# Routing of a product-key expert layer: one span of gather slots for each head, a second buffer for transposed h, and w_out's products in smaller steps through the gather's row buffers

## The chip, the cores and the metric

The kernel runs on one core of a Trainium2 chip, as one launch. The metric is the device time of that launch in microseconds (us), as the median of several executions. One execution was also profiled; the rows in this document come from it.

## The reference, cut to what matters

256 tokens (two tiles of 128) of 1024 channels go through two layers. Each layer mixes the tokens in four ways (short convolution, latent attention, a 31-tap convolution, windowed attention), multiplies by `w_out`, normalises to `h`, and then sends every token to 128 of 16384 experts:

```python
m = per_head_rms_norm(concat[shortconv, MLA, conformer_conv, swa](x @ W_in))
h = layer_norm(ALPHA * x + m @ W_out)
x = layer_norm(ALPHA * h + PEER(h))

def PEER(xc):                                   # 8 heads, 16 experts a head and token
    q = (xc @ w_q).reshape(c, 8, 2, 128)
    sc = einsum('chpd,hpnd->chpn', q, sub_keys)             # two times 128 scores
    top_s, top_i = top_k(sc, 16)
    best_s, best_j = top_k(top_s[:, :, 0, :, None] + top_s[:, :, 1, None, :], 16)
    idx = the expert of each best pair
    gate = softmax(best_s)
    act = gelu(einsum('chkd,cd->chk', u_tab[idx], xc))
    return einsum('chk,chkd->cd', gate * act, v_tab[idx])
```

All of it is float32.

## The kernel before, in words

**The gather.** `u` and `v` of an expert lie side by side in a row of 2048 floats. For each tile of each layer (a stage: four in all, `todo`) the function `peer` (L734) runs 128 *slots*, 16 for each head. A slot gathers 128 rows, one for each token: 1 MB by an indirect DMA that GpSimd (POOL) issues (L756) into one of ten row buffers (`ROWS`, tag `row`). VectorE (DVE) multiplies the u half with `h` and sums (L759), ScalarE (ACT) takes the gelu, the gate and a diagonal matrix `dg` (L741 to L744), and TensorE (PE) adds `dg` times the v half to two accumulators `acc` (L746). `post` of a slot is written after the DVE step of the next slot. A row buffer is free when PE has read it.

**The routing.** `route` (L660) makes the 16 experts and gates of one head: two times eight products `ps_q` of transposed `h` with the head's weights `w_q_t` (1152 KB), a product `ps_rs` with the keys, then top-16 searches and index arithmetic on DVE (`top16`, `sum_grid`, `experts`). Heads 0 to 2 keep their weights from the first tile to the second in `held0` to `held2`; heads 3 and 4 are loaded for each tile; heads 5 to 7 are loaded once and routed for both tiles in one go (`joint`, L797). For that the transposed `h` of the first tile is made a second time, in the buffer `pT`, and the second tile begins its gather with heads 5 to 7.

**The mixers.** `mixer` (L286) makes `h` of one tile. At its end `outs` (L572) loads four blocks of `w_out` (1 MB each) and makes 16 products `ps_o` (L586), and a layer norm follows. Weights go through the pool `wp` of three buffers, filled by SP's DMA queue in the order in which a scheduler puts the loads.

**Who sets the order.** `paced` (L822) emits the slots of a stage one after another, and between them steps of other *tasks*. A task is a generator with a first and a last slot and a cost; each `yield` says what it has spent, and a task is stepped until it has spent its share for the slot. `main_loop` (L866) lists the tasks of each stage: routing in rows such as `(joint(0), 65, 100, ...)`, which means that six routes (three heads for two tiles) are spread over slots 65 to 100, and mixers such as `(mix(1, 1), 4, 66, MIX)`. `keep_behind` ties the two streams together: on PE, DVE and ACT a task's step comes at most six slots before or behind its place. The order within that is a scheduler's.

The stages are, with the tasks beside the gather:

| stage | gather of | routing beside it, slots | mixer beside it, slots |
|---|---|---|---|
| 1 | layer 1, tile 1 | head 1: 0-4; heads 2 to 4: 4-17; joint 5 to 7: 65-100 | layer 1, tile 2: 0-65 |
| 2 | layer 1, tile 2 | heads 0 to 4: 2-36; next layer's 0, 1: 104-120 | layer 2, tile 1: 36-104 |
| 3 | layer 2, tile 1 | heads 2 to 4: 3-17; joint 5 to 7: 66-101 | layer 2, tile 2: 4-66 |
| 4 | layer 2, tile 2 | heads 0 to 4: 2-70 | none |

(The code counts layers and tiles from 0.) Ahead of stage 1 lie the first mixer and the first route; behind stage 4 the last layer norm.

Of the kernel before, what the change touches and what calls it, by code (L numbers as in the profile page):

```python
# [61 lines left out]
def kernel(ctx: ExitStack, tc: tile.TileContext, x, positions, w_in, w_att, bcast, perch, lnrows, lncols,  # L62
# [597 lines left out]
    def route(l, hd, hTs):  # L660

        n = QK
        if hd in HELD and 1 in hTs:
            w = held.pop(hd)
        else:
            if hd in HELD:
                held[hd] = rp.tile([P, n], F32, tag=f"held{hd}", name="w_q_t")
            w = load_w(w_qk, (l * NH + hd) * P * n, n, "w_q_t", held.get(hd))
        wq = w[:, :KC * 256].rearrange("p (c n) -> p c n", c=KC)
        for t, hT in hTs.items():  # L670
            s = []
            for j in range(2):
                ps = pm.tile([P, P], F32, tag="mm", name="ps_q")
                for c in range(KC):
                    nc.tensor.matmul(ps, wq[:, c, j * P:(j + 1) * P], hT[:, c, :], start=(c == 0), stop=(c == KC - 1))  # L675
                yield 1.8
                qT = sp.tile([P, P], F32, tag=f"rq{j}", name="rq", bufs=1)
                S.copy(qT, ps)  # L678
                ps = pm.tile([P, P], F32, tag="mm", name="ps_rs")
                nc.tensor.matmul(ps, qT, w[:, KC * 256 + j * P:KC * 256 + (j + 1) * P], start=True, stop=True)  # L680
                s.append(sp.tile([P, P], F32, tag=f"rsc{j}", name="rsc", bufs=1))
                S.copy(s[j], ps)  # L682
                yield 0.3
            bs = sp.tile([P, TOPK], F32, tag="bs", name="bs")
            bj = sp.tile([P, TOPK], U32, tag="bj", name="bj")
            ix8 = None
            if (l, t, hd) == (0, 0, 0):

                t8 = sp.tile([P, 2, TOPK], F32, tag="tv", name="t8")
                i8 = sp.tile([P, 2, TOPK], U32, tag="ti", name="i8")  # L690
                for j in range(2):
                    V.max(t8[:, j, 0:8], s[j])
                    V.max_index(i8[:, j, 0:8], t8[:, j, 0:8], s[j])
                c8 = sum_grid(t8, 8)
                b8 = sp.tile([P, 8], F32, tag="b8", name="b8", bufs=1)
                j8 = sp.tile([P, 8], U32, tag="j8", name="j8", bufs=1)
                V.max(b8, c8)
                V.max_index(j8, b8, c8)
                ix8 = gp.tile([P, 8], I32, tag="ix8", name="ix8", bufs=1)
                experts(l, ix8, j8, i8, 8, 8)  # L700
            tv = sp.tile([P, 2, TOPK], F32, **(dict(tag="ex0", bufs=1) if (l, t) == (0, 0) and hd < HS else dict(tag="tv")),
                         name="tv")
            ti = sp.tile([P, 2, TOPK], U32, tag="ti", name="ti")
            for j in range(2):
                top16(tv[:, j, :], ti[:, j, :], s[j])
                yield 1.0
            top16(bs, bj, sum_grid(tv, TOPK))
            yield 2.0
            ix = gp.tile([P, TOPK], I32, tag=f"ix{hd}", name="ix", bufs=2)
            experts(l, ix, bj, ti, TOPK, TOPK)  # L710
            yield 2.2

            nb = sp.tile([P, 1], F32, tag="nb", name="nb")
            V.tensor_scalar(nb, bs[:, 0:1], -1.0 / 16, None, op0=ALU.mult)
            th = sp.tile([P, TOPK], F32, tag="th", name="th")
            S.activation(th, bs, AF.Tanh, bias=nb, scale=1.0 / 16)
            tm = sp.tile([P, TOPK], F32, tag="tm", name="tm")
            V.tensor_scalar(tm, th, -1.0, 1.0, op0=ALU.mult, op1=ALU.add)
            V.reciprocal(tm, tm)
            V.scalar_tensor_tensor(tm, th, 1.0, tm, op0=ALU.add, op1=ALU.mult)  # L720
            sm = sp.tile([P, 1], F32, tag="gsm", name="gsm")
            gate = gp.tile([P, TOPK], F32, tag=f"gate{hd}", name="gate", bufs=2)
            S.activation(tm, tm, AF.Square)
            S.activation(tm, tm, AF.Square)
            S.activation(gate, tm, AF.Square, accum_out=sm)
            V.reciprocal(sm, sm)
            V.tensor_scalar(gate, gate, sm, None, op0=ALU.mult)
            R[l, t, hd] = (ix8, ix, gate)
            yield 0.5
# [56 lines left out]

    def solo(l, t, heads):

        if t == 0 and not hot["pT"]:
            hot["pT"] = transpose8(H[l, 0], "hT0", "pT")  # L790
            yield 1.5
        for hd in heads:
            yield from route(l, hd, {t: hot["T"] if t else hot["pT"]})
        if t == 0 and hd == HS - 1:
            hot["pT"] = 0

    def joint(l):  # L797

        hot["T"] = transpose8(H[l, 1], "hT1", "T")
        yield 1.5  # L800
        hT0 = transpose8(H[l, 0], "hT0", "pT")
        yield 1.5
        for hd in range(HS, NH):
            yield from route(l, hd, {0: hT0, 1: hot["T"]})
# [164 lines left out]
```

## Time and profile before

| what | value |
|---|---|
| time before, median of 3 runs (lowest to highest) | 1544.36 us (1543.88 to 1546.22) |
| the profiled execution's own time | 1543.23 us |
| its span, first to last instruction | 1541.2 us |
| busy: PE, DVE, POOL, ACT | 87%, 71%, 40%, 38% |
| moved by DMA | 614.47 MB, 399 GB/s over the span |
| of this the gather | 512 indirect DMAs, 536.90 MB |

Busy shares are means over stretches that have different limits. [...]

### The profile page before, as it was taken

How to read it: one execution, taken by the hardware profiler on the slowest of the kernel's cores; microseconds unless marked ns; L12 is line 12 of the kernel's file. 1: busy time of each engine (PE TensorE's matmuls, PEld its weight loads, DVE VectorE, ACT ScalarE, POOL GpSimd, SP SyncE). 2: the span in 40 equal slices, each digit the busy share in tenths (PEclk: the TensorE clock that was granted, in tenths of full speed). 3: DMA queues.
4: the chain of work that ended last, by engine and by line, in shares of the span. 5: the costliest groups of instructions: out<-in, count | busy, mean ns of one | idle time of the engine just before them, and what ended most of it. 6: DMA issues, size and time to landing. Idle time of an engine off the chain costs nothing.

```text
span 1541.2 us, 17548 instructions
## 1 busy us (share of the span) xinstructions
PE 1345.3 (87%) x4868; PEld 720.2 (47%) x4868; DVE 1096.8 (71%) x3163; ACT 589.6 (38%) x2047; POOL 618.4 (40%) x539
## 2 busy tenths in 40 slices
PE   8999889798989789978989999898988898888776
PEld 8676444454335455533444665444543444432222
DVE  6789785699659775677487787757984777665445
ACT  4234442343434333354243334423443343433332
POOL 2044233234654233434335334232445454555551
PEclk9999899999999999999999999899999999999999
DMA  9579999999999999999999999999999999999995
GB/s 381 195 319 421 418 393 401 416 385 405 420 421 422 422 422 423 422 422 384 424 381 422 422 423 422 378 420 363 374 396 422 421 422 421 421 421 422 421 421 239
DMA packets 86209, 614.47 MB, mean 399 GB/s; under 512 B 10337, under 2 KB 10721, under 8 KB 12769
## 3 DMA queue, kind: packets, MB, share of 16 engines
q0 software_dynamic: 73728, 536.90, 84.9%
q1 hardware_dynamic: 12096, 76.44, 12.1%
q8 instruction: 40, 0.66, 0.2%
q14 instruction: 57, 0.46, 0.1%
q10 hardware_dynamic: 288, 0.01, 0.0%
HBM read 612.26 MB, written 1.05 MB: 398 GB/s over the span
## 4 chain that ended last, share of the span: by engine, by line
PE 39%; DMA 28%; DVE 22%; issue 6%; ACT 4%; POOL 0%; DVEq 0%; SPq 0%; POOLq 0%
DMA row<-in_uv_dram,ix 27%; PE acc L746 26%; DVE row L759 9%; PE ps_q L675 5%; PE ps_o L586 3%; DVE cv L510 1%; DMA w_in_t<-in_w_in_dram 1%; ACT dg L744 1%; PE ps_mla L320 1%; DVE bj L655 1%; DVE rsc L656 1%; DVE ti L655 1%; DVE grid L656 1%; DVE ti L658 1%; ACT act L742 1%
## 5 line engine op out<-in xcount | busy, mean ns | idle before, releaser
L746 PE MATMUL acc<-row,dg 128*128 128x512 f32 x2048 | 987.2, 615 | 162.0 <-ACT dg L744 160.8
L756 POOL DMA_INDIRECT row<-in_uv_dram,ix x512 | 607.4, 1186 | 866.0 <-PE acc L746 299.4
L759 DVE SCALAR_TENSOR_TENSOR row<-row,h 128x1024 f32<-128x1024 f32 x512 | 619.2, 1219 | 225.8 <-DMA row<-in_uv_dram,ix 201.2
L746 PEld LDWEIGHTS acc<-row,dg 128*128 128x128 f32 x2048 | 366.1, 193 | 643.7 <-ACT dg L744 331.9
L741 ACT ACTIVATE act<-act 128x1 f32<-128x1 f32 x512 | 103.1, 201 | 581.5 <-DVE row L759 580.7
L744 ACT ACTIVATE dg<-idn,act 128x128 f32<-128x128 f32 x512 | 205.1, 401 | 72.5 <-PE acc L746 58.5
L742 ACT ACTIVATE act<-act,gate 128x1 f32<-128x1 f32 x512 | 150.2, 294 | 15.5
L675 PEld LDWEIGHTS ps_q<-hT,w_q_t 128*128 128x128 f32 x1024 | 124.6, 194 | 23.3 <-issue 22.2
L675 PE MATMUL ps_q<-hT,w_q_t 128*128 128x128 f32 x1024 | 128.6, 278 | 5.8 <-DVE hp L153 5.6
L510 DVE SCALAR_TENSOR_TENSOR cv<-cfu,pc,cv 128x128 f32<-128x128 f32 x217 | 68.7, 358 | 0.9
L586 PE MATMUL ps_o<-w_out_t,mT 128*128 128x512 f32 x128 | 61.7, 615 | 1.7 <-DVE mT L370 1.7
L654 DVE MAX8 tv<-rsc 128x8 f32<-128x128 f32 x64 | 18.4, 289 | 46.8 <-ACT rsc L682 46.5
L682 ACT COPY rsc<-ps_rs 128x128 f32<-128x128 f32 x64 | 17.0, 265 | 66.7 <-PE ps_rs L680 66.4
L759 DVE DVE_READ_ACCUMULATOR row<-row,h 128x1 f32 x512 | 41.9, 82 | 0.0
L586 PEld LDWEIGHTS ps_o<-w_out_t,mT 128*128 128x128 f32 x128 | 24.7, 198 | 31.2 <-issue 28.7
L680 PEld LDWEIGHTS ps_rs<-w_q_t,rq 128*128 128x128 f32 x128 | 23.6, 190 | 29.4 <-issue 22.2
L592 DVE SCALAR_TENSOR_TENSOR hp<-x,ps_o 128x512 f32<-128x512 f32 x8 | 5.5, 687 | 38.5 <-PE ps_o L586 38.5
L678 ACT COPY rq<-ps_q 128x128 f32<-128x128 f32 x64 | 16.8, 262 | 39.7 <-PE ps_q L675 39.5
L680 PE MATMUL ps_rs<-w_q_t,rq 128*128 128x128 f32 x128 | 25.1, 278 | 2.1 <-ACT rq L678 2.1
L320 PEld LDWEIGHTS ps_mla<-w_in_t,xT 128*128 128x128 f32 x128 | 23.4, 196 | 4.0 <-issue 2.9
L320 PE MATMUL ps_mla<-w_in_t,xT 128*128 128x208 f32 x128 | 24.9, 348 | 0.2 <-DMA w_in_t<-in_w_in_dram 0.2
L649 DVE TENSOR_REDUCE ex<-grid 128x32 f32<-128x512 f32 (+1 forms) x33 | 22.0, 667 | 0.3
(215 smaller groups left out, 977.9 us busy)
## 6 DMA issues: line engine op xcount, KB each, us to landing
w_in_t<-in_w_in_dram SPq DMA_DIRECT2D x24, 1024.0 KB, 10.1
w_q_t<-in_w_qk_dram SPq DMA_DIRECT2D x20, 1152.0 KB, 9.4
w_out_t<-in_w_out_dram SPq DMA_DIRECT2D x16, 1024.0 KB, 10.4
row<-in_uv_dram,ix POOLq DMA_INDIRECT x512, 16.5
w_in_t<-in_w_in_dram SPq DMA_DIRECT2D x6, 832.0 KB, 7.9
att<-in_w_att_dram SPq DMA_DIRECT2D x2, 640.0 KB, 12.7
x<-in_x_dram SPq DMA_DIRECT2D x2, 512.0 KB, 6.7
gb<-in_lnrows_dram SPq DMA_DIRECT2D x1, 1024.0 KB, 13.6
```

Source lines behind the costliest of these rows:

```text
L320: nc.tensor.matmul(ps, xT[:, c, :], w[:, c, a:b], start=(c == 0), stop=(c == KC - 1))
L510: V.scalar_tensor_tensor(cv[j], src, wt, cv[j], op0=ALU.mult, op1=ALU.add)
L586: nc.tensor.matmul(po[j], mixed_T()[:, 2 * g + c, :], wg[:, c, j * 512:(j + 1) * 512], start=(n == 0 and c == 0), stop=(n == 3 and c == 1))
L655: V.max_index(idx[:, 0:8], val[:, 0:8], s)
L675: nc.tensor.matmul(ps, wq[:, c, j * P:(j + 1) * P], hT[:, c, :], start=(c == 0), stop=(c == KC - 1))
L680: nc.tensor.matmul(ps, qT, w[:, KC * 256 + j * P:KC * 256 + (j + 1) * P], start=True, stop=True)
L741: S.activation(act, act, AF.Gelu)
L742: S.activation(act, act, AF.Copy, scale=gate[:, k % TOPK:k % TOPK + 1])
L744: S.activation(dg, idn, AF.Copy, scale=act)
L746: nc.tensor.matmul(acc[j], dg, row[:, DM + j * 512:DM + (j + 1) * 512], start=(k == 0), stop=(k == n - 1))
L756: nc.gpsimd.indirect_dma_start(out=row, out_offset=None, in_=uv, in_offset=bass.IndirectOffsetOnAxis(ap=ix[:, k % TOPK:k % TOPK + 1], axis=0))
L759: V.scalar_tensor_tensor(row[:, :DM], row[:, :DM], 1.0, h, op0=ALU.mult, op1=ALU.mult, accum_out=act)
```

## The change

- `route` takes one tile and one head. `joint` and `solo` are gone. Each head of each tile is a task of its own with its own span of slots. In stages 1 and 3 the first tile's heads follow each other at some 16 slots each, the mixer beside them; from slot 80 the second tile's heads 5 to 7 and the first tile's head 7 follow.
- The weights of heads 5 to 7 are kept in the three `wp` buffers from the first tile's route to the second's (`KEPT`). So the number of loads stays (20 of `w_q_t`, 16 of `w_out_t`, 30 of `w_in_t`).
- Transposed `h` is made once for each tile, in the tag `T`, which has two buffers.
- The four `w_out` blocks of the later mixers go into row buffers of the gather instead of `wp`, and `outs` yields after each product: 16 steps of 1.7 instead of 8. `MIX` is raised by 14 accordingly.
- To make room four small tiles share tags with others (`gsq` with `cT`, `pes` with `scc`, `sq` with `sg`, `tap` with `dg`).

The diff, cut to its core:

```diff
-HS = 5
+HELD = (0, 1, 2)
+KEPT = (5, 6, 7)
+HEADS = ((0, 1, 2, 3, 4, 5, 6, 7), (5, 6, 7, 0, 1, 2, 3, 4))
-MIX, ROUTE, TAIL = 97.0, 10.9, 6.6
+MIX, ROUTE, TAIL = 111.0, 10.9, 6.6
-    def transpose8(src, name, tag="T", act_only=False):
-        d = mp.tile([P, KC, P], F32, tag=tag, name=name)
+    def transpose8(src, name, act_only=False):
+        d = mp.tile([P, KC, P], F32, tag="T", name=name, bufs=2)
...
-                    wo[g] = w_out_rows(g)
+                    wo[g] = w_out_rows(g, gp.tile([P, 2 * DM], F32, tag="row", name="w_out_t"))
...
                         nc.tensor.matmul(po[j], mixed_T()[:, 2 * g + c, :], wg[:, c, j * 512:(j + 1) * 512],
                                          start=(n == 0 and c == 0), stop=(n == 3 and c == 1))
+                        if c == 0:
+                            yield 1.7
...
-    def route(l, hd, hTs):
+    def route(l, t, hd):
         n = QK
-        if hd in HELD and 1 in hTs:
-            w = held.pop(hd)
-        else:
+        w = held.pop((l, hd), None)
+        if w is None:
             if hd in HELD:
-                held[hd] = rp.tile([P, n], F32, tag=f"held{hd}", name="w_q_t")
-            w = load_w(w_qk, (l * NH + hd) * P * n, n, "w_q_t", held.get(hd))
+                w = rp.tile([P, n], F32, tag=f"held{hd}", name="w_q_t")
+            w = load_w(w_qk, (l * NH + hd) * P * n, n, "w_q_t", w)
+            if t == 0 and hd in HELD + KEPT:
+                held[l, hd] = w
...
-        for t, hT in hTs.items():
+        if (l, t) not in HT:
+            HT[l, t] = transpose8(H[l, t], f"hT{t}")
+            yield 1.5
+        hT = HT[l, t]
...
+    def routes(l, t, spans):
+        return [(route(l, t, hd), a, b, ROUTE) for hd, (a, b) in spans.items()]
...
+            tasks = [(tail, 0, 3, TAIL)] if i else []
+            if t == 0:
+                tasks += routes(l, 0, {1: (0, 3)} if l == 0 else {})
+                tasks += routes(l, 0, {2: (0, 17), 3: (17, 32), 4: (32, 48), 5: (48, 64), 6: (64, 80)})
+                tasks += [(mix(1, 1) if l else ahead, 0 if l == 0 else 3, 80, MIX)]
+                tasks += routes(l, 1, {5: (80, 94)}) + routes(l, 0, {7: (84, 97)}) + routes(l, 1, {6: (97, 112), 7: (112, 128)})
             else:
-                tasks = [(tail, 0, 3, TAIL), (solo(1, 1, range(HS)), 2, 70, HS * ROUTE)]
+                tasks += routes(l, 1, {0: (3, 20), 1: (20, 38), 2: (38, 56), 3: (56, 74), 4: (74, 92)})
+                if l == 0:
+                    tasks += [(mix(1, 0), 3, 98, MIX)] + routes(1, 0, {0: (98, 112), 1: (112, 126)})
```

Since the scheduler decides the final order, three places of it are shown. `acc x2` is one slot of the gather on PE. First PE at the end of stage 3's mixer, where `ps_o` are the products with `w_out`; before:

```order
L586 MATMUL ps_o<-w_out_t,mT 128x512 x2
L746 MATMUL acc<-row,dg 128x512 x2
L586 MATMUL ps_o<-w_out_t,mT 128x512 x2
L746 MATMUL acc<-row,dg 128x512 x4
L586 MATMUL ps_o<-w_out_t,mT 128x512 x2
L369 MATMUL ps_mT<-idn,m 128x128 x2
L746 MATMUL acc<-row,dg 128x512 x2
L586 MATMUL ps_o<-w_out_t,mT 128x512 x2
```

and with the change:

```order
L585 MATMUL ps_o<-w_out_t,mT 128x512 x4
L680 MATMUL ps_q<-hT_5616,w_q_t 128x128 x8
L750 MATMUL acc<-row,dg 128x512 x4
L685 MATMUL ps_rs<-w_q_t,rq 128x128
L750 MATMUL acc<-row,dg 128x512 x2
L680 MATMUL ps_q<-hT_5616,w_q_t 128x128 x8
L750 MATMUL acc<-row,dg 128x512 x2
L585 MATMUL ps_o<-w_out_t,mT 128x512 x4
L750 MATMUL acc<-row,dg 128x512 x2
L685 MATMUL ps_rs<-w_q_t,rq 128x128
L750 MATMUL acc<-row,dg 128x512 x8
L585 MATMUL ps_o<-w_out_t,mT 128x512 x4
```

Before, two products stood before nearly every slot; now four stand together, five or six slots apart, and a head's products lie between.

Second, PE in stage 3 behind the mixer; `hT_7679` and `hT_7666` are the first and the second tile's transposed h in `joint` before:

```order
L746 MATMUL acc<-row,dg 128x512 x6
L675 MATMUL ps_q<-hT_7666,w_q_t 128x128 x8
L746 MATMUL acc<-row,dg 128x512 x2
L680 MATMUL ps_rs<-w_q_t,rq 128x128
L675 MATMUL ps_q<-hT_7666,w_q_t 128x128 x8
L746 MATMUL acc<-row,dg 128x512 x2
L680 MATMUL ps_rs<-w_q_t,rq 128x128
L746 MATMUL acc<-row,dg 128x512 x6
L675 MATMUL ps_q<-hT_7679,w_q_t 128x128 x8
```

and with the change (`hT_5616` is the first tile's, `hT_7951` the second's):

```order
L680 MATMUL ps_q<-hT_5616,w_q_t 128x128 x6
L750 MATMUL acc<-row,dg 128x512 x2
L680 MATMUL ps_q<-hT_5616,w_q_t 128x128 x2
L750 MATMUL acc<-row,dg 128x512 x2
L685 MATMUL ps_rs<-w_q_t,rq 128x128
L750 MATMUL acc<-row,dg 128x512 x18
L680 MATMUL ps_q<-hT_7951,w_q_t 128x128 x8
L750 MATMUL acc<-row,dg 128x512 x4
L685 MATMUL ps_rs<-w_q_t,rq 128x128
```

Before, a route began every five or six slots; now, after a pair at slots 80 to 97, the next begins some nine slots behind the last.

Third, DVE in stage 3 at the latent attention's softmax (`S_mla` its scores, `mx` their maximum, `tv` and `ti` a head's best scores and their places); before:

```order
L247 TENSOR_TENSOR S_mla<-ps_s,maskt 128x2x128
L521 TENSOR_TENSOR ct<-ct,bc 128x256
L252 TENSOR_REDUCE mx<-S_mla 128x4
L522 TENSOR_TENSOR ct<-ct,bc 128x256
L370 TENSOR_TENSOR mT<-ps_mT,pc 128x256
L759 SCALAR_TENSOR_TENSOR row,act<-row,h 128x1024
```

and with the change:

```order
L250 TENSOR_TENSOR S_mla<-ps_s,maskt 128x2x128 x2
L655 MAX tv<-rsc 128x8
L111 SCALAR_TENSOR_TENSOR rs_y<-rs_u,rs_y 128x4
L373 TENSOR_TENSOR mT<-ps_mT,pc 128x256
L255 TENSOR_REDUCE mx<-S_mla 128x4
L656 MAX_INDEX ti<-tv,rsc 128x8
L109 TENSOR_TENSOR rs_u<-rs_y 128x4
L763 SCALAR_TENSOR_TENSOR row,act<-row,h 128x1024
```

Before, the mixer had this stretch of DVE for itself; now a head's search lies in it.

## Rows read from the trace of the kernel before

**Rows 1.** The page: busy us by engine, and GB/s in 40 equal slices.

```profile
PE 1345.3 (87%) x4868; PEld 720.2 (47%) x4868; DVE 1096.8 (71%) x3163; ACT 589.6 (38%) x2047; POOL 618.4 (40%) x539
...
GB/s 381 195 319 421 418 393 401 416 385 405 420 421 422 422 422 423 422 422 384 424 381 422 422 423 422 378 420 363 374 396 422 421 422 421 421 421 422 421 421 239
```

**Rows 2.** Windows, start, gather, end: stretch, length, busy us (instructions), clock, DMA share, GB/s.

```profile
0.00:100.00 100.00, 89.58 (x580) 74.83 (x581) 67.89 (x288) 33.38 (x95) 19.73 (x35) 0.97 0.71 280
100.00:1520.00 1420.00, 1246.21 (x4272) 642.24 (x4271) 1017.04 (x2850) 552.64 (x1940) 598.70 (x504) 0.98 1.00 412
1520.00:1541.20 21.20, 9.49 (x20) 3.09 (x18) 11.85 (x27) 3.59 (x12) 0.00 (x0) 0.85 0.23 92
```

**Rows 3.** Windows (busy: PE, PEld, DVE, ACT, POOL), the six stretches below full rate.

```profile
220.00:260.00 40.00, 38.74 (x108) 18.26 (x107) 25.55 (x66) 15.10 (x53) 15.68 (x15) 0.99 0.97 372
300.00:360.00 60.00, 53.26 (x228) 31.49 (x227) 54.56 (x180) 25.80 (x101) 22.23 (x21) 1.00 0.97 383
700.00:740.00 40.00, 36.04 (x90) 16.10 (x91) 26.45 (x69) 18.37 (x59) 15.47 (x14) 0.96 0.97 386
780.00:820.00 40.00, 34.81 (x105) 16.44 (x105) 36.74 (x99) 18.80 (x70) 18.78 (x16) 1.00 0.98 384
980.00:1020.00 40.00, 40.00 (x109) 18.98 (x108) 25.27 (x65) 15.26 (x50) 14.08 (x13) 0.93 0.95 377
1040.00:1160.00 120.00, 104.39 (x395) 57.17 (x396) 100.44 (x313) 50.38 (x193) 47.37 (x43) 1.00 0.97 379
```

**Rows 4.** Windows, seven stretches at or near full rate, the last with the gather alone.

```profile
100.00:160.00 60.00, 60.00 (x297) 39.62 (x296) 52.90 (x199) 23.93 (x93) 25.88 (x23) 1.00 1.01 421
160.00:220.00 60.00, 48.04 (x162) 25.38 (x161) 50.77 (x168) 28.78 (x90) 17.12 (x16) 0.86 1.01 419
640.00:700.00 60.00, 46.17 (x144) 21.76 (x142) 45.40 (x139) 27.06 (x80) 23.25 (x20) 0.94 1.01 422
920.00:980.00 60.00, 51.35 (x190) 28.45 (x189) 47.40 (x151) 28.21 (x85) 24.88 (x20) 0.93 1.01 422
460.00:560.00 100.00, 82.82 (x314) 46.00 (x315) 83.33 (x272) 36.58 (x142) 34.94 (x32) 0.95 1.01 422
1200.00:1380.00 180.00, 155.99 (x493) 74.06 (x492) 134.22 (x347) 71.04 (x258) 89.29 (x71) 1.00 1.01 421
1400.00:1500.00 100.00, 78.95 (x161) 26.94 (x160) 48.98 (x81) 35.92 (x120) 55.21 (x40) 1.00 1.01 421
```

**Rows 5.** Windows, the mixers' ends up to their first product with w_out.

```profile
220.00:234.00 14.00, 12.74 (x46) 6.69 (x45) 10.91 (x37) 5.37 (x18) 6.24 (x6) 0.97 0.93 329
...
705.00:720.00 15.00, 14.05 (x38) 6.51 (x39) 10.94 (x39) 5.70 (x19) 6.68 (x5) 0.89 0.92 342
...
980.00:995.00 15.00, 15.00 (x49) 7.82 (x48) 10.06 (x28) 7.00 (x21) 5.15 (x5) 0.82 0.84 321
```

**Rows 6.** Timeline 972 to 992: start, us, engine, line, operation [idle before <- releaser].

```profile
975.36 1.28 ACT L262 ACT_TABLE_LOAD   x1
...
979.26 6.74 PE L746 MATMUL acc<-row,dg 128*128 128x512 f32 x8 [6.52 <-ACT dg L744]
...
983.31 1.41 POOL L756 DMA_INDIRECT row<-in_uv_dram,ix  x1 [9.59 <-PE acc L746]
```

**Rows 7.** Chain that ended last, 240 to 280: start, us, what (PE passes).

```profile
255.59 8.58 PE acc L746 x20
...
265.04 3.45 PE ps_o L586 x8
```

**Rows 8.** Line L756, all its gathers: from issue to landing.

```profile
DMA to landing us min/median/max: 5.4/16.5/25.8
```

**Rows 9.** Timeline of POOL, 86 to 110: the eighth and the ninth gather.

```profile
97.57 1.11 POOL L756 DMA_INDIRECT row<-in_uv_dram,ix  x1 [0.30 <-issue]
104.60 0.94 POOL L756 DMA_INDIRECT row<-in_uv_dram,ix  x1 [5.92 <-PE acc L746]
```

**Rows 10.** DMA issues of the page: KB each, median us to landing.

```profile
w_q_t<-in_w_qk_dram SPq DMA_DIRECT2D x20, 1152.0 KB, 9.4
w_out_t<-in_w_out_dram SPq DMA_DIRECT2D x16, 1024.0 KB, 10.4
```

More of the change, by code (lines that the diff above doesn't have):

```diff
@@ L356, in group @@
             mg = m[g]
-            sq = mp.tile([P, 256], F32, tag="gsq", name="gsq")
+            sq = mp.tile([P, 256], F32, tag="cT", name="gsq")
             S.activation(sq, mg, AF.Square)
@@ L669, in route @@
         wq = w[:, :KC * 256].rearrange("p (c n) -> p c n", c=KC)
-        for t, hT in hTs.items():
-            s = []
-            for j in range(2):
[L673 to L729, printed above, removed]
@@ L731 @@
-    R, held = {}, {}
-    HELD = (0, 1, 2)
+        if (l, t) not in HT:
+            HT[l, t] = transpose8(H[l, t], f"hT{t}")
+            yield 1.5
+        hT = HT[l, t]
+        s = []
+        for j in range(2):
+            ps = pm.tile([P, P], F32, tag="mm", name="ps_q")
+            for c in range(KC):
+                nc.tensor.matmul(ps, wq[:, c, j * P:(j + 1) * P], hT[:, c, :], start=(c == 0), stop=(c == KC - 1))
+            yield 1.8
+            qT = sp.tile([P, P], F32, tag=f"rq{j}", name="rq", bufs=1)
+            S.copy(qT, ps)
+            ps = pm.tile([P, P], F32, tag="mm", name="ps_rs")
+            nc.tensor.matmul(ps, qT, w[:, KC * 256 + j * P:KC * 256 + (j + 1) * P], start=True, stop=True)
+            s.append(sp.tile([P, P], F32, tag=f"rsc{j}", name="rsc", bufs=1))
+            S.copy(s[j], ps)
+            yield 0.3
@@ new lines, in route @@
+        tv = sp.tile([P, 2, TOPK], F32, **(dict(tag="ex0", bufs=1) if (l, t) == (0, 0) and hd < KEPT[0] else dict(tag="tv")),
+                     name="tv")
+        ti = sp.tile([P, 2, TOPK], U32, tag="ti", name="ti")
+        for j in range(2):
+            top16(tv[:, j, :], ti[:, j, :], s[j])
+            yield 1.0
+        top16(bs, bj, sum_grid(tv, TOPK))
+        yield 2.0
+        ix = gp.tile([P, TOPK], I32, tag=f"ix{hd}", name="ix", bufs=2)
+        experts(l, ix, bj, ti, TOPK, TOPK)
@@ new lines, in route @@
+        yield 2.2
+        nb = sp.tile([P, 1], F32, tag="nb", name="nb")
+        V.tensor_scalar(nb, bs[:, 0:1], -1.0 / 16, None, op0=ALU.mult)
+        th = sp.tile([P, TOPK], F32, tag="th", name="th")
+        S.activation(th, bs, AF.Tanh, bias=nb, scale=1.0 / 16)
+        tm = sp.tile([P, TOPK], F32, tag="tm", name="tm")
+        V.tensor_scalar(tm, th, -1.0, 1.0, op0=ALU.mult, op1=ALU.add)
+        V.reciprocal(tm, tm)
+        V.scalar_tensor_tensor(tm, th, 1.0, tm, op0=ALU.add, op1=ALU.mult)
@@ L734, in peer @@
+        sm = sp.tile([P, 1], F32, tag="gsm", name="gsm")
+        gate = gp.tile([P, TOPK], F32, tag=f"gate{hd}", name="gate", bufs=2)
+        S.activation(tm, tm, AF.Square)
+        S.activation(tm, tm, AF.Square)
+        S.activation(gate, tm, AF.Square, accum_out=sm)
+        V.reciprocal(sm, sm)
+        V.tensor_scalar(gate, gate, sm, None, op0=ALU.mult)
+        R[l, t, hd] = (ix8, ix, gate)
+        yield 0.5
+    R, held, HT = {}, {}, {}
     def peer(l, t, h, acc):
         n = NH * TOPK
-        order = list(range(HS, NH)) + list(range(HS)) if t else list(range(NH))
+        order = HEADS[t]
@@ L785, in mix @@
         H[l, t] = yield from mixer(l, t, Y[l], X[t])
[L787 to L804, printed above, removed]
     log = nc.cur_bb.bb.instructions
@@ L862 @@
                 next(ahead)
-    for _ in solo(0, 0, [0]):
+    for _ in route(0, 0, 0):
         pass
+    def routes(l, t, spans):
+        return [(route(l, t, hd), a, b, ROUTE) for hd, (a, b) in spans.items()]
     def main_loop():
```

37 lines of the change are left out of this document (19 added, 18 removed).

## Prediction, before the changed kernel was run

> **What bounds the kernel now.** The page's slices come first [rows 1]: PE is busy 87% of the span, yet the slices that stand at 420 to 424 GB/s, 24 of 40, whatever the engines do in them, say that the transfers set the pace. With the gather alone the same rate holds [rows 4]: 161 PE passes in 100 us, four a slot, are 2.485 us a slot, PE busy 79 of 100 us, DVE 49. So time is lost where the rate falls below 422 GB/s. The windows by phase [rows 2] put that loss at three places: the start up to 100 us, the end from 1520 us, and between them 412 instead of 422 GB/s over 1420 us, which is 1420 x 10/422 = 33.6 us. The change has nothing to do at the start and the end: it moves the same bytes, the first route is unchanged, and the last stage ends with the gather alone. It can win no more than these 34 us, unless bytes fall.
>
> Finer windows find the 34 us in six stretches [rows 3]; each costs its length x (422 - rate)/422.
>
> - The two joint routings, 300 to 360 and 1040 to 1160 us: 5.5 + 12.2 = 17.8 us. DVE is busy 54.6 of 60 and 100.4 of 120 us there.
> - Two heads in 16 slots behind the second mixer, 780 to 820 us: 3.6 us, DVE 36.7 of 40.
> - The ends of the three mixers, from 220, 700 and 980 us: 4.7 + 3.4 + 4.3 = 12.4 us. They belong to two causes. Up to the first product with w_out [rows 5] they lose 14 x 93/422 + 15 x 80/422 + 15 x 101/422 = 9.5 us. The timeline shows why [rows 6]: ACT loads a table and makes the softmax's exponentials, the gather's own `dg` waits behind them, PE idles 6.5 us, and the gather's next issue waits 9.6 us for a buffer. Only the other 2.9 us fall where PE runs `ps_o`.
>
> **The change, part by part.** The sum starts from the profiled execution, 1543.2 us.
>
> *Routes apart.* The 180 us in which the last stage routes five heads against the gather alone [rows 4]: (134.2 - 1.8 x 49.0)/5 = 9.2 us of DVE a route, and 49.0/40.25 = 1.22 us a slot for the gather. In the joint stretch six routes stand on 35 slots: 35 x 1.22 + 6 x 9.2 = 97.9 us of DVE, against 35 x 2.485 + three loads of 1152 KB at 422 GB/s [rows 10] (8.4 us) = 95.4 us of transfers. DVE is the bound there, and its waits in the chain come on top. With one route on 16 slots it is 28.7 of 39.8 us. That alone runs at full rate: five routes stood on 34 slots, without a mixer, at 460 to 560 us with 422 GB/s [rows 4]. So the 17.8 us and the 3.6 us go: -21.4. The transposes of h that go (eight a layer) were in the same stretches and are counted with them.
>
> *The pair at slots 80 to 97.* In stages 1 and 3 two routes lie on 17 slots right behind a mixer, as they did at 780 us. Each costs between 0 and the 3.6 us of that stretch; PE has less beside it now (no next projections), so I take the middle: 2 x 1.8 = +3.6.
>
> *w_out.* The order shows that the finer steps do not reach PE: products stand in fours. What changes is the distance, one four in five to seven slots. A four takes 3.45 us [rows 7]; PE needs 4 x 0.43 = 1.72 us a slot [rows 7], so six slots leave 6 x (2.485 - 1.72) = 4.6 us for it. The 2.9 us go: -2.9. The bounds are 0 and -2.9; I take the full amount because nothing else in that stretch wants much of PE but a route's products.
>
> *Row buffers.* The gather's ten buffers now also carry w_out. A block lands in 10.4 us [rows 10], and its four stands in the built program eight or nine slots behind the one whose buffer it takes, so one or two of ten are away at a time. Eight are enough: at the start the gather had eight, its ninth issue waited 5.9 us for PE [rows 9], and from 100 us the rate is 421 [rows 4]. With an empty queue a row lands in 5.4 us [rows 8] and needs about 6.3 us more on DVE, ACT and PE including the slot that `post` is behind: 12 us, five slots. Cost 0; the cover is the three spare rows, some 7 us of stall, and without it each stall is lost in full.
>
> *Routes beside the mixers.* This is the new cost. In the 60 us ahead of each softmax DVE is busy 50.8, 45.4 and 47.4 us and the rate is still full [rows 4]. Now a route on 16 slots adds 60/(16 x 2.85) = 1.3 routes, 12 us: 63, 57 and 59 of 60. (The mixers are also paced some 7 to 18% slower, which takes a few us off.) Nearest rows: 52.9 of 60 with no loss [rows 4], 54.6 of 60 with 5.5 us lost [rows 3]. So each softmax, which keeps its own 3 us of loss, costs between 0 and 5.5 us more; I take a third, 3 x 1.8 = +5.5, because the queue is full when it begins.
>
> *Nothing for the rest.* ACT gets 20 table loads in the order where there were 18; the two are 2 x 1.28 = 2.6 us [rows 6] on an engine busy 38% [rows 1]; if they fall before a `dg`, they are part of the 5.5. The shared tags of small tiles add waits inside a mixer that has 77 to 95 slots. SP's loads are as many as before, and the 9 to 10 us of their landing [rows 10] are four slots.
>
> Sum: 1543.2 - 21.4 + 3.6 - 2.9 + 5.5 = 1528.0. The median shown is 1.1 us above the profiled execution, so **1529 us**.
>
> [...] PE's granted clock is 1.00 with the gather alone, its thinnest load [rows 4], and 0.82 to 0.97 after each softmax, where PE has idled 6.5 us [rows 5, 6]; 160 to 220 us, at 0.86, still moved 419 GB/s [rows 4]. [...]
>
> **The rivals.**
>
> *Nothing comes back beside the mixers.* DVE full for 60 us is absorbed by the queue, and the pairs cost nothing: 1543.2 - 21.4 - 2.9 + 1.1 = 1520 us. For it: 100 to 160 us. Against: the softmax stretches already lose with no route beside them. If even the softmaxes lost nothing, 1511.
>
> *The loss only moves.* Each mixer's end loses the joint stretch's 5.5 us more and each pair the full 3.6: 16.5 + 7.2 = 23.7, against 24.3 won: 1544 us, no change. For it: the same DVE work, and the third place of the order, where a head's search stands between scores and maximum. It decides if DVE is late by more than the spare rows hold in all three.
>
> *Half clock in the w_out stretch: slower.* The four fours of a tile span some 25 slots. At full clock PE needs 25 x 1.72 + 4 x 3.45 = 57 us for them, the transfers 25 x 2.485 + 4 x 2.5 = 72 us. [...] Against it: the lowest mean clock of these rows is 0.82, over 15 us [rows 5]. For it: fewer spare rows make each ACT burst reach PE sooner, and PE then works on at half clock.
>
> *The change doesn't do what it says* holds for the steps of w_out in part, as said; it is in the sum.
>
> **How the numbers follow.** Forecast 0.45, nothing comes back 0.20, loss moves 0.20, half clock 0.15. The low end lies between the second case and the one without any loss: 1514. The high end takes in the moved loss and the mild part of the half clock: 1546. Runs of this kernel differ by about 0.15%, so 0.2% (3 us) is what can be told from no change: faster is below 1541.3. Most of the first two cases and a fifth of the third is faster: 0.45 x 0.95 + 0.20 + 0.04 = 0.67, and 0.03 of the last case's mild part: 0.70. Same: half of the third and a little of the first, 0.13. The rest is slower, 0.17.
>
> **What would show it.** Right: 421 to 423 GB/s where heads 5 to 7 are routed, PE's `ps_o` in fours with gather between, and dips that remain at the three softmaxes and small ones at slots 80 to 97. Wrong: a dip in slots 16 to 48 of stages 1 to 3 (DVE full), POOL waiting for `ps_o` (rows short), a mean clock below 0.75 over a w_out stretch, or SP late with a load so that PE waits for `w_q_t` or `w_out_t`.

## The result, and the profile after

The kernel after takes 1521.55 us, the median of 4 runs (1520.31 to 1524.16); the kernel before took 1544.12 us beside it (4 runs, 1542.98 to 1546.22). The ratio is 0.9855, with a 95% interval of 0.9837 to 0.9872: faster by 22.6 us, 20 to 25. The prediction said 1529 us and 1514 to 1546. So the sign and the range held, but the gain is 7 us more than the sum, and the profile shows at once that the sum missed something. The profiled execution took 1520.93 us, its span is 1518.9 us.

From the page of the kernel after: busy us by engine, GB/s in 40 equal slices, and the median landing of a w_out block.

```profile
PE 1336.2 (88%) x4852; PEld 714.6 (47%) x4852; DVE 1096.7 (72%) x3161; ACT 590.1 (39%) x2047; POOL 632.3 (42%) x539
...
GB/s 383 177 324 426 426 428 396 385 401 424 426 426 427 426 426 427 420 389 426 427 427 426 427 426 427 411 334 407 419 426 428 426 427 426 427 427 427 427 427 220
...
w_out_t<-in_w_out_dram SPq DMA_DIRECT2D x16, 1024.0 KB, 6.2
```

The engines do what they did [rows 1]. But the slices at the top of the row, which stood at 420 to 424 GB/s [rows 1], now stand at 424 to 428. **The full rate itself has risen by 1.2%.** The prediction took it for fixed.

Windows of the kernel after (busy us of PE, PEld, DVE, ACT, POOL, then the granted share of PE's full clock, DMA share, GB/s). First the two places of the joint routings and the gather alone, then the three softmaxes, the three w_out stretches, the pairs of routes, and the 60 us ahead of the second softmax.

```profile
340.00:460.00 120.00, 104.72 (x328) 50.24 (x327) 91.87 (x249) 49.10 (x180) 60.25 (x50) 1.00 1.01 426
1100.00:1200.00 100.00, 88.73 (x287) 43.68 (x288) 75.97 (x191) 43.27 (x159) 50.27 (x42) 1.00 1.01 427
1380.00:1480.00 100.00, 80.33 (x164) 27.63 (x162) 56.06 (x111) 37.47 (x128) 55.52 (x40) 1.00 1.01 427
...
220.00:260.00 40.00, 37.23 (x127) 19.42 (x127) 27.03 (x87) 16.24 (x54) 14.73 (x12) 0.94 0.99 398
640.00:680.00 40.00, 35.55 (x100) 16.60 (x99) 30.26 (x93) 14.54 (x52) 15.73 (x13) 0.94 0.99 389
960.00:1000.00 40.00, 35.77 (x149) 21.49 (x150) 36.00 (x138) 22.05 (x67) 9.90 (x10) 0.96 0.90 355
260.00:300.00 40.00, 35.17 (x106) 16.95 (x105) 25.80 (x71) 14.21 (x54) 14.46 (x13) 1.00 0.98 389
1000.00:1040.00 40.00, 36.60 (x110) 17.53 (x109) 26.86 (x77) 13.64 (x51) 12.85 (x13) 1.00 0.97 378
680.00:720.00 40.00, 38.88 (x103) 17.88 (x102) 25.24 (x65) 15.35 (x57) 19.75 (x18) 1.00 1.01 425
320.00:340.00 20.00, 18.82 (x83) 11.60 (x84) 15.06 (x39) 9.88 (x36) 10.19 (x8) 1.00 0.98 376
1080.00:1100.00 20.00, 17.50 (x56) 8.29 (x54) 18.44 (x66) 7.04 (x27) 8.96 (x9) 1.00 1.00 412
580.00:640.00 60.00, 46.45 (x149) 23.14 (x148) 50.35 (x170) 32.90 (x100) 22.67 (x19) 0.93 1.01 425
```

The gather alone runs at 427 where it ran at 421 [rows 4]: there PE, the busiest engine, works 80 of the 100 us, and of the changed work only one head's search is left (DVE 56 against 49 us in 100). The stretches that held the joint routings run at full rate now; before they were at 383 and 379 [rows 3]. What is left, as length x (427 - rate)/427: at the softmaxes 2.7 + 3.6 + 6.7 = 13.0 us, at w_out 3.6 + 4.6 = 8.2 us, at the pairs 2.4 + 0.7 = 3.1 us, in all 24.3 us. The third w_out stretch, from 680 us, loses 0.2. Before it was 33.6 us of 422 [rows 2]. So the dips gave back some 9 us and the rate the rest: 614.47 MB take 1456.1 us at 422 GB/s and 1439.0 us at 427, 17 us less. (The column is rounded to 1 GB/s, which is 3 us over the whole gather; the experiments measure the two shares by times.)

These windows are of one execution. A second profiled execution of the same kernel, the run `after_again` below, has other rates in some of them:

```profile
220.00:260.00 40.00, 36.99 (x130) 19.12 (x128) 28.17 (x89) 15.48 (x54) 15.71 (x13) 0.98 1.01 415
260.00:300.00 40.00, 35.42 (x107) 17.41 (x107) 23.49 (x64) 13.63 (x51) 14.16 (x14) 1.00 0.99 405
320.00:340.00 20.00, 20.00 (x91) 12.38 (x90) 13.57 (x32) 8.86 (x34) 10.18 (x8) 1.00 0.98 370
960.00:1000.00 40.00, 36.56 (x151) 22.04 (x152) 36.12 (x140) 21.47 (x68) 10.64 (x11) 0.96 0.88 334
```

At 640 to 680 us it has 382, at 1000 to 1040 us 377, and the same dips add up to 23.6 us. So the sum holds, but a single softmax window, or the one at 260 to 300 us, can differ by some 20 GB/s between executions of one kernel, and smaller differences there tell nothing.

### The profile page after: what moved, and what is told of

Same layout as the page of the kernel before. It is cut to its first block, busy times and chain, and to the rows that moved or that the text cites. A ratio compares the mean times of both kernels' runs of the same rounds, so it can differ in the third digit from the quotient of the medians.

```text
span 1518.9 us, 17527 instructions
## 1 busy us (share of the span) xinstructions
PE 1336.2 (88%) x4852; PEld 714.6 (47%) x4852; DVE 1096.7 (72%) x3161; ACT 590.1 (39%) x2047; POOL 632.3 (42%) x539
## 2 busy tenths in 40 slices
DMA packets 86208, 614.47 MB, mean 405 GB/s; under 512 B 10336, under 2 KB 10720, under 8 KB 12768
## 4 chain that ended last, share of the span: by engine, by line
PE 41%; DMA 31%; DVE 17%; ACT 5%; issue 4%; POOL 0%; DVEq 0%; POOLq 0%; SPq 0%; ACTq 0%
DMA row<-in_uv_dram,ix 31%; PE acc L750 24%; DVE row L763 7%; PE ps_q L680 6%; PE ps_o L585 3%; DVE cv L509 2%; ACT dg L748 1%; PE ps_cfa L319 1%; PE ps_mla L323 1%; ACT act L746 1%; PE ps_rs L685 1%; PE ps_scb L319 1%; ACT act L745 1%; PE po L284 1%; ACT L265 1%
## 5 line engine op out<-in xcount | busy, mean ns | idle before, releaser
L760 POOL DMA_INDIRECT row<-in_uv_dram,ix x512 | 621.1, 1213 | 830.0 <-PE acc L750 272.5
L649 DVE TENSOR_TENSOR grid<-tf,ab 128x512 f32<-128x512 f32 (+1 forms) x33 | 22.3, 674 | 0.6
```

What stands on the lines that cost most here:

```text
L760: nc.gpsimd.indirect_dma_start(out=row, out_offset=None, in_=uv, in_offset=bass.IndirectOffsetOnAxis(ap=ix[:, k % TOPK:k % TOPK + 1], axis=0))
```

## The experiments

Two questions. Why did the full rate rise? And what did the change's own parts bring, place by place? All times are medians beside the kernel before on the same chip (1544.1 to 1545.1 us).

### Why the rate rose: the place of the row buffers

The second buffer for `T` takes 4096 bytes of a partition more, and the shared tags give back 3712; the difference, 384 bytes, shifts what is allocated behind them. In the built programs the ten row buffers begin at byte 142,720 of a partition before, which is 128 past a multiple of 256, and at byte 143,104 after, which is a multiple of 256. Each buffer takes 8192 bytes, so all ten share the offset. That is theory A. It can be tried without touching any work: one small tile ahead of them is made larger.

```diff
-b8 = sp.tile([P, 8], F32, tag="b8", name="b8", bufs=1)
+b8 = sp.tile([P, 40], F32, tag="b8", name="b8", bufs=1)[:, :8]
```

That is 128 bytes more. It moves the row buffers and the small tiles behind `b8` (indices, gates, `dg` among them); the other buffers that weights are loaded into lie ahead of it and stay. It was made in the kernel before and in the kernel after; with 24 columns the offset of the kernel after becomes 64, with 72 columns it is a multiple of 512. The two unchanged kernels ran beside the first pair (the kernel before was also profiled once more, in 1545.7 us).

> The kernel before with one small tile made 128 bytes larger, so that the ten row buffers start at a multiple of 256 bytes in a partition, as in the kernel after (before, they started 128 bytes past one). Nothing else moves; the order on every engine is the same. Theory A (the buffers' place sets the full rate): the gather alone runs at 426 to 428 GB/s instead of 421 to 422 and the time falls by about 1.2% of 1420 us, to 1526 to 1531 us. Rival B (the chip, or where the tables lie in DRAM, sets it): the rate is that of the kernel before on this chip and the time 1544. Rival C (the changed kernel's own work beside the gather raises the rate): 422 GB/s and 1544.

> The kernel after with the same 128 bytes added, so that its row buffers start 128 bytes past a multiple of 256, as before. Theory A: the gather alone at 421 to 422 GB/s and 1535 to 1540 us; what is left against the kernel before, 5 to 9 us, is what the routes and w_out's steps bring. Rivals B and C: 426 to 428 GB/s and 1521 to 1523 us.

> The kernel after unchanged, on the same chip as its fellows. All theories: near 1521.5 us; the rate of the gather alone is read beside that of the kernel before on this chip. Theory A expects 426 to 428 GB/s, rival B the rate of the kernel before.

> The kernel before unchanged, for a profile on the same chip. Theory A: 421 to 422 GB/s with the gather alone and 1544 us. Rival B: the same rate as the other three kernels, whatever it is.

> The kernel after with 64 bytes more, so that its row buffers start 64 bytes past a multiple of 256. If any place off a multiple of 256 costs the same: 421 to 422 GB/s with the gather alone and 1534 to 1538 us, as at 128. If only the half (128) costs: 426 to 428 and 1520. If smaller offsets cost less or more: a rate between or below.

> The kernel after with 256 bytes more ahead of the row buffers, so that they start at a multiple of 512 instead of 256 past one. If a multiple of 256 is what counts: 426 to 428 GB/s with the gather alone and 1519 to 1522 us. If the rate goes on rising with the alignment: 429 GB/s or more and some 5 us less. If neither, but the exact place in a partition counts: another rate, either way.

| row buffers start at, past a multiple of 256 bytes | kernel | time, us | ratio to before, 95% interval | gather alone, GB/s |
|---|---|---|---|---|
| 128 | before | 1544.1 | 1 | 422 |
| 0 | before, moved | 1533.1 | 0.9928 (0.9915 to 0.9941) | 427 |
| 128 | after, moved | 1535.61 | 0.9940 (0.9928 to 0.9952) | 421 |
| 64 | after, moved | 1536.57 | 0.9944 (0.9929 to 0.9959) | 421 |
| 0 | after | 1520.41 | 0.9845 (0.9831 to 0.9859) | 427 |
| 0 (of 512 too) | after, moved | 1519.3 | 0.9844 (0.9828 to 0.9860) | 427 |

Windows with the gather alone, and of the two joint stretches with some us around them, for the kernel before:

```profile
1020.00:1180.00 160.00, 140.15 (x496) 73.19 (x495) 121.07 (x354) 61.37 (x228) 67.48 (x60) 1.00 0.98 390
280.00:400.00 120.00, 107.26 (x408) 58.95 (x409) 102.28 (x317) 51.69 (x193) 47.36 (x43) 0.99 0.99 403
1380.00:1480.00 100.00, 79.54 (x162) 27.23 (x161) 49.86 (x81) 35.93 (x120) 55.22 (x41) 1.00 1.01 422
```

and for the kernel before with its row buffers moved:

```profile
1020.00:1180.00 160.00, 138.63 (x484) 71.27 (x483) 125.05 (x361) 62.99 (x233) 68.24 (x59) 1.00 0.98 390
280.00:400.00 120.00, 107.26 (x411) 59.02 (x411) 101.17 (x314) 50.91 (x191) 49.24 (x44) 0.99 0.99 401
1380.00:1480.00 100.00, 80.34 (x163) 27.56 (x163) 50.30 (x81) 35.92 (x120) 55.48 (x41) 1.00 1.01 427
```

for the kernel after with them at 128, and then at 64:

```profile
1380.00:1480.00 100.00, 81.74 (x197) 31.59 (x196) 57.06 (x117) 37.24 (x128) 55.38 (x40) 1.00 1.01 421
```

```profile
1380.00:1480.00 100.00, 81.95 (x198) 31.83 (x197) 57.64 (x117) 37.02 (x129) 55.02 (x41) 1.00 1.01 421
```

All lines of the table but the fourth ran on one chip. In the last window the engines are busy as they were, only the rate moves, and it follows the offset in both kernels. So rivals B and C fall. 128 and 64 cost the same, and a multiple of 512 brings no more than one of 256: as far as these four places show, what counts is whether the start is a multiple of 256. The small tiles that move along were not tried apart from the row buffers; that the row buffers are the cause is the nearest reading, since of what moves only they are filled by the transfers.

The table also parts the change. At the old offset it is worth 1544.1 - 1535.6 = 8.5 us (by the ratio 9.3, 7.4 to 11.1). The offset alone is worth 11.0 us in the kernel before and 15.2 in the kernel after, where theory A expected some 16 in both, so its range was missed in the kernel before (1533.1 against 1526 to 1531). The joint stretches offer a reason: there the rate is 390 GB/s at either offset, and 403 or 401, so it does not follow the offset; that DVE, busy 100.4 of 120 and 54.6 of 60 us at their core [rows 3], sets the pace instead is the prediction's estimate. If these 280 us have no part in the 1.2%, that is 3.3 of the 4.2 us between 11.0 and 15.2, a difference that only just clears the intervals.

### w_out's steps undone

```diff
-MIX, ROUTE, TAIL = 111.0, 10.9, 6.6
+MIX, ROUTE, TAIL = 97.0, 10.9, 6.6
...
-                        if c == 0:
-                            yield 1.7
```

> The kernel after without the extra step of outs, and MIX at 97 as before: w_out's fours then stand three slots apart instead of five. The prediction's term (distance between fours is what counts) expects the 2.9 us back: 1523. Theory W expects more, 1523 to 1527, since routes lie in the same slots. Rival S expects 1519 to 1522.

1523.04 us, ratio 0.9861 (0.9845 to 0.9877), so 2.6 us slower than the kernel after, with intervals that overlap: the size that the prediction's term had, not proven. PE's order in stage 1 still has fours, some three slots apart. MIX at 97 also moves the mixer: its first product with w_out there comes at 276 instead of 257 us. So the 2.6 us are not the price of the distance alone.

### w_out loaded one block ahead

```diff
                 if not start:
-                    wo[g] = w_out_rows(g, gp.tile([P, 2 * DM], F32, tag="row", name="w_out_t"))
+                    for f in order[n:n + 2]:
+                        if f not in wo:
+                            wo[f] = w_out_rows(f, gp.tile([P, 2 * DM], F32, tag="row", name="w_out_t"))
```

> The kernel after, with each w_out block of the later mixers loaded one block earlier (the next block's load is written before the present block's products). In PE's order the products then stand singly, a slot or two apart, instead of in fours; two row buffers instead of one are away for a time. Theory W (the fours on PE, on top of a head's products, hold ACT's and DVE's order up): the dips behind the softmax, 280 to 300 us (2.0 us) and 1000 to 1040 us (4.6 us), close and the time falls from 1520.4 by 4 to 6 us, to 1514 to 1516. Rival R (row buffers are what is short): POOL waits longer for acc or ps_o in these stretches and the time is 1522 to 1526. Rival S (what costs is the softmax beside a route, and w_out nothing): 1519 to 1522, the dip at 980 to 1000 us as before it.

1519.67 us, ratio 0.9837 (0.9821 to 0.9853): no difference from the kernel after that can be told. Its windows, stage 1's w_out and pair, then the other two mixers' ends:

```profile
260.00:300.00 40.00, 37.19 (x112) 18.34 (x112) 24.96 (x63) 14.07 (x51) 17.86 (x15) 1.00 1.01 418
320.00:340.00 20.00, 19.46 (x102) 13.09 (x101) 12.59 (x31) 8.13 (x29) 6.85 (x8) 1.00 1.00 419
580.00:640.00 60.00, 48.05 (x152) 23.88 (x153) 50.39 (x175) 33.20 (x101) 22.01 (x19) 0.94 1.00 406
960.00:1000.00 40.00, 37.22 (x151) 22.20 (x149) 34.42 (x137) 19.84 (x62) 10.97 (x10) 0.92 0.85 328
1000.00:1040.00 40.00, 37.29 (x113) 18.21 (x113) 22.93 (x63) 13.24 (x49) 12.97 (x15) 1.00 0.96 380
```

Theory W is right in stage 1: with the products spread, 389 and 405 in the two executions of the kernel after become 418 and, behind it, 376 and 370 become 419. So the dip at the pair of routes was mostly the queue that w_out's fours had emptied. In stage 3 it is wrong: 378 and 380 are the same, so the fours alone do not make that dip. Its time is missed too; 1519.67 lies where rival S put it, though S gave w_out no cost. The loss of 3.0 us at 580 to 640 is new (425 before); why is not shown, since w_out's first load in that stage begins at 645 us. 328 at 960 to 1000 is no news beside 334.

### Stage 3's mixer end without routes

```diff
-                tasks += routes(l, 0, {2: (0, 17), 3: (17, 32), 4: (32, 48), 5: (48, 64), 6: (64, 80)})
+                tasks += routes(l, 0, {2: (0, 17), 3: (17, 32), 4: (32, 48), 5: (48, 64), 6: (64, 80)} if l == 0 else
+                                {2: (0, 12), 3: (12, 24), 4: (24, 36), 5: (36, 48)})
...
+                else:
+                    tasks += routes(l, 0, {6: (80, 89)}) + routes(l, 1, {5: (89, 99)}) + routes(l, 0, {7: (99, 109)}) + routes(l, 1, {6: (109, 119), 7: (119, 128)})
```

> The kernel after, with stage 3's heads moved: heads 2 to 5 of the first tile at 12 slots each (0 to 48), none beside the mixer's end (48 to 80), and the remaining five routes at 9 to 10 slots each behind it (80 to 128). Theory S (a route beside the softmax and w_out is what costs): the 13 us lost from 960 to 1040 us fall to the 4 to 5 us that this mixer's end lost before the change, and the time to 1511 to 1514. Rival D (DVE's work only moves: four routes beside the mixer in 48 slots, five behind it): new dips before and behind take it back, 1519 to 1526.

1515.12 us, ratio 0.9815 (0.9801 to 0.9829): 5.3 us faster than the kernel after, and the intervals do not meet; theory S had expected 1 to 4 us more. Its windows: the softmax, w_out, and the denser routes behind it.

```profile
960.00:1000.00 40.00, 36.26 (x121) 18.47 (x119) 36.37 (x133) 22.19 (x69) 12.65 (x11) 0.92 0.87 333
1000.00:1040.00 40.00, 38.88 (x89) 16.47 (x88) 18.64 (x32) 14.22 (x48) 20.99 (x17) 1.00 1.01 426
1060.00:1160.00 100.00, 89.41 (x314) 46.28 (x313) 81.81 (x231) 41.79 (x156) 43.69 (x41) 1.00 1.01 427
```

The w_out stretch goes from 378 to 426, although its products still stand in fours and PE is busier than in the kernel after (38.9 against 36.6 of 40 us). So neither the fours by themselves nor PE's load is the cost, but a head's route among them. The run takes away the route's steps on all engines at once; how they cost is read from the timeline of the kernel after (start, us, engine, operation, idle before and releaser):

```profile
1023.42 1.95 PE L680 MATMUL ps_q<-hT,w_q_t 128*128 128x128 f32 x16
1025.21 1.88 PE L750 MATMUL acc<-row,dg 128*128 128x512 f32 x4
1025.41 0.27 ACT L683 COPY rq<-ps_q 128x128 f32<-128x128 f32 x1 [2.15 <-PE ps_q L680]
...
1026.92 3.60 PE L585 MATMUL ps_o<-w_out_t,mT 128*128 128x512 f32 x8
1030.36 1.88 PE L750 MATMUL acc<-row,dg 128*128 128x512 f32 x4
1032.08 0.38 PE L685 MATMUL ps_rs<-w_q_t,rq 128*128 128x128 f32 x2
1032.50 0.27 ACT L687 COPY rsc<-ps_rs 128x128 f32<-128x128 f32 x1 [6.39 <-PE ps_rs L685]
1032.80 0.30 DVE L655 MAX8 tv<-rsc 128x8 f32<-128x128 f32 x1 [5.98 <-ACT rsc L687]
```

ACT has copied `rq`, which `ps_rs` needs, at 1025.7 us, but PE comes to `ps_rs` only at 1032.1: a four (x8, two passes a product) and two of the gather's slots stand ahead of it. ACT reaches its copy of `ps_rs` and waits 6.39 us, with the gather's `dg` behind it (at 1032.7 us); DVE reaches the search that wants the copy and waits 5.98 us, with the gather's next rows behind it (at 1034.8 us). So a head's step holds up the gather on ACT and on DVE: PE is busy, but DVE works 26.9 of 40 us. ACT's waits for `ps_rs` from 1000 to 1040 us (us, times, longest), in the kernel after and with w_out one block ahead:

```profile
ACT rsc L687 <- PE ps_rs L685: 9.4, 2, 6.4
ACT rsc L689 <- PE ps_rs L687: 9.8, 2, 5.1
```

They are as long where the products are spread, which fits the equal rates (378 and 380); without routes there are none. One such wait alone is covered: from 680 to 720 us in the kernel after ACT waits 4.7 us for `ps_rs` once, and the rate is 425. The denser routes behind the mixer cost nothing (427), so rival D is wrong there. The dip at the softmax stays (333, beside 355 and 334), which theory S did not expect.

### Nine row buffers

```diff
-ROWS = 10
+ROWS = 9
```

> The kernel after with nine row buffers instead of ten, at the same first address. The prediction gave the row buffers that w_out borrows no cost, because eight are enough: then one fewer costs next to nothing where no mixer's end lies (427 GB/s stays with the gather alone) and at most 1 to 3 us at the three mixers' ends: 1520 to 1524. Theory R (each spare buffer is worth its 2.45 us at every stall of the gather, and there are some eight stalls): 8 to 15 us more, 1528 to 1536.

1526.36 us, ratio 0.9894 (0.9879 to 0.9909): 6.0 us slower than the kernel after (7.6 by the ratios), between the two expectations.

```profile
220.00:260.00 40.00, 36.69 (x130) 19.11 (x130) 27.23 (x89) 14.72 (x52) 15.86 (x14) 0.99 0.97 366
640.00:680.00 40.00, 33.83 (x97) 16.02 (x96) 27.71 (x80) 13.71 (x49) 14.82 (x13) 0.95 0.93 359
960.00:1000.00 40.00, 33.11 (x128) 18.84 (x128) 32.76 (x117) 19.51 (x63) 11.82 (x11) 0.96 0.86 316
1380.00:1480.00 100.00, 81.44 (x181) 29.43 (x179) 57.31 (x117) 37.27 (x128) 41.04 (x42) 1.00 1.01 427
```

With the gather alone nine are as good as ten (427). The softmaxes lose more: 398 and 415 in the two executions of the kernel after become 366, 389 and 382 become 359, 355 and 334 become 316, which is 1.7 to 4.6 us each. The last of these is not certain: the kernel with its rows at a multiple of 512 has 302 there. At w_out little changes (405, 427 and 371 GB/s, from 260, 680 and 1000 us).

### The edits together

First all at once: w_out one block ahead, stage 3's heads 2 to 5 at 10 slots each, and stage 2's routes moved as well:

```diff
+                                {2: (0, 10), 3: (10, 20), 4: (20, 30), 5: (30, 40)})
...
+                    tasks += routes(l, 1, {0: (3, 17), 1: (17, 31), 2: (31, 45), 3: (45, 59), 4: (98, 107)})
+                    tasks += [(mix(1, 0), 3, 98, MIX)] + routes(1, 0, {0: (107, 117), 1: (117, 127)})
```

> The kernel after with three edits together: w_out one block ahead; stage 3 as in the run with its mixer's end alone, but heads 2 to 5 at 10 slots each (0 to 40), so that their DVE work is over before the softmax; stage 2 likewise (heads 0 to 3 at 14 slots each up to slot 59, head 4 and the next layer's two behind the mixer, 98 to 127). Theory Q (a softmax costs its full 5 to 9 us where DVE's work of a route right ahead of it has emptied the queue, and some 4 us where not): the dip at 980 to 1000 us falls from 7.5 to about 4, the one at 640 to 680 us from 4.2 to about 3, stage 1's w_out dip closes: 1515 less 3, 1 and 3, so 1507 to 1510. Rival D (work moved into denser stretches is lost there): 1513 to 1520. Rival M (the softmax dip of stage 3 is the mixer's own, whatever lies ahead of it): 7 us stay at 960 to 1000 us and the time is 1511 to 1513.

1514.97 us, ratio 0.9818 (0.9804 to 0.9831): rival D.

```profile
580.00:640.00 60.00, 45.01 (x147) 22.90 (x146) 48.77 (x161) 32.43 (x99) 22.17 (x18) 0.94 0.98 394
960.00:1000.00 40.00, 34.70 (x120) 18.30 (x119) 31.68 (x106) 22.62 (x70) 12.48 (x12) 0.96 0.92 359
1000.00:1040.00 40.00, 38.78 (x91) 16.68 (x90) 21.33 (x47) 12.86 (x45) 15.05 (x15) 1.00 0.98 395
```

With DVE at 31.7 instead of 36.0 of 40 us stage 3's softmax still loses 40 x 68/427 = 6.4 us, so theory Q's price of some 4 us for an uncrowded softmax is not met; that dip is as rival M has it, the time is not. Stage 2, with its routes at 14 slots instead of 18, now loses 60 x 33/427 = 4.6 us from 580 to 640, where the kernel after is at 425 GB/s; 3.0 of them were lost there with w_out one block ahead alone.

Then only the two edits that each had closed a dip: w_out ahead in stage 1 (`order[n:n + (2 if (l, t) == (0, 1) else 1)]`), and stage 3 as in the run of its mixer's end alone.

> The kernel after with the two edits at the places where each one's own run closed a dip: w_out one block ahead in stage 1 alone, and stage 3's heads as in the run with its mixer's end alone. If the losses are local and add up: stage 1 from 240 to 340 us loses some 3 instead of 6 us as in the run with w_out ahead, 1000 to 1040 us runs at 426 GB/s as in the run with stage 3's mixer's end alone (1515.1 us), so 1511 to 1513. If what one place wins is lost at the next: 1514 to 1517.

1515.12 us (1509.52 to 1516.11), ratio 0.9801 (0.9784 to 0.9817).

```profile
260.00:300.00 40.00, 38.53 (x116) 18.80 (x114) 24.71 (x64) 13.18 (x48) 17.50 (x15) 1.00 1.00 406
320.00:340.00 20.00, 19.46 (x86) 11.76 (x85) 13.53 (x34) 8.08 (x30) 8.05 (x8) 1.00 1.00 405
960.00:1000.00 40.00, 35.11 (x117) 18.50 (x117) 35.09 (x128) 21.18 (x65) 11.74 (x11) 0.91 0.85 319
1000.00:1040.00 40.00, 39.54 (x91) 16.74 (x89) 19.68 (x34) 14.86 (x50) 20.95 (x17) 1.00 1.01 426
```

Two gains are there: 405 instead of 376 and 370 at stage 1's pair, and 426 instead of 378 at stage 3's w_out. 406 from 260 to 300 us is none, since the kernel after has 405 there in its second execution. The time is the second expectation's, that what one place wins is lost at the next; where it is lost is not shown: 319 at the softmax of stage 3 is 3.4 us beside 355, but 1.4 beside 334. It beats both kernels, 1.8 to 2.2% below the kernel before, but cannot be told from the run with stage 3's edit alone.

## Why the prediction was right, and where it was wrong

**The bound.** That transfers set the pace held, and so did the places of the loss. The step that failed is the sentence "It can win no more than these 34 us, unless bytes fall": it took 422 GB/s for the chip's rate. It was the rate of row buffers 128 bytes off. This missing term is worth 15.2 us in the kernel after. Without it the change would stand at 1535.6 us, 6.6 above the forecast and still within the range. So the number came out on the right side through two errors of opposite sign, and the rival that named 1520 us (nothing comes back) was near it for a wrong reason: 24 us of dips are there.

**Routes apart, -21.4: right.** 383, 379 and 384 GB/s [rows 3] became 426 and 427 at the joint places, and 427 in the run with five routes on 48 slots.

**The pairs, +3.6: the size right (3.1), the reason not.** 2.4 of it is in stage 1, and all but 0.4 of that goes when w_out's products are spread (419; 405 where only stage 1's are): the queue had been emptied ahead of the pair.

**w_out, -2.9: wrong by its cover.** The fours came as the order showed, and the clock stayed at 1.00 there. But 8.2 us (6.8 in the second execution) are lost in two of those stretches instead of none; only stage 2's, where a head's products lie ahead of the second four alone, loses next to none (425). The step that failed is "nothing else in that stretch wants much of PE but a route's products". The prediction counted PE's time (it has enough: 36.6 of 40 us, and 38.9 at full rate), not the order: a head's scores wait behind what stands ahead of them on PE, fours and the gather's own slots, and ACT and DVE wait for those scores (6.4 and 6.0 us in the timeline above), the gather's steps behind them. Taking the routes out of stage 3's stretch gave 5.3 us; spreading the fours there gave nothing.

**Row buffers, 0: too small.** "Eight are enough" holds for the steady gather: nine give 427. It does not hold for a stall. One buffer is worth 6.0 us in all, most of it at the softmaxes. A sign of being wrong that the prediction named did come: POOL waits for `ps_o`, which in the kernel before it never does.

```profile
POOL row L760 <- PE ps_o L585: 27.2, 10, 4.3
```

Some of these waits lie at full rate (680 to 720 us), so they are no price. What the borrowing itself costs was not tried: with heads 5 to 7 kept there is no other room for the blocks.

**Routes beside the mixers, +5.5 on 9.5: about right as a sum (13.0 against 15.0), unevenly spread.** Two softmaxes are about as before, the third loses 6.7 (8.7 in the second execution) instead of about 3.6 us. The assumed cause, DVE's queue full from a route, is not shown: with less DVE work it still lost 6.4. Why this softmax is dearer than before the change stays open.

**Half clock: did not come.** No run shows the term that the chances (0.15) and the high end of the range use, the cost of a half clock over a w_out stretch. In the kernel after the clock is 1.00 from 260 to 300 and from 1000 to 1040 us, with fours and holes between, and 0.94 to 0.96 over the softmaxes. Half clock shows in short stretches, as at the first softmax: from 219.0 to 224.5 us the mean is 0.50, after PE idled 4.2 us, and eight of the gather's passes take 6.46 us, against 3.60 at a clock of 1.00 (from 1017.1 us). From 260 to 300 us PE never idles longer than 1.4 us, so no longer idle time beside w_out was tried there.

## What to carry to other kernels

Before a rate is taken for the chip's limit, look where the destination buffers lie: here 128 bytes in an unrelated tile moved every buffer behind it, and the rate from 422 to 427 GB/s. Vary that offset in both kernels whenever a change touches allocation, or its effect is booked to something else. And a piece of work is not hidden because its engine has time left: here PE was busy 36.6 of 40 us, and ACT waited 6.4 us for a head's scores. Look at what stands behind it in the order, on the engines that wait for it.

## What the runs showed of the hardware

The gather of 8 KB rows ran, alone, at 427 GB/s where its row buffers start at a multiple of 256 bytes in a partition (`before_rows_at_256`, `after_again`, `after_rows_at_512`), and at 421 to 422 where they start 64 or 128 bytes past one (`after_rows_at_64`, `after_rows_at_128`, `before_again`); in time 11.0 us of 1544 and 15.2 us of 1536. No other places were tried, and no run here moved the source. Why the start counts is not shown.
